# First layer's scales and shifts by packed matmuls with the weights moving, and the first value tiles projected beside the keys

## The chip, the core and the metric

The kernel runs on one core of a Trainium2 chip. The metric is the device time of one execution in microseconds; before the change it is 1470.97 us, the median of three runs (1470.38 to 1471.1).

## The reference, cut to what matters

Two layers over 1024 latent tokens and 256 context tokens of width 1024. Each layer scales and shifts its tokens by vectors made from a conditioning vector (`c` for the latents, `c_ctx` for the context), projects them, attends, gates, projects back and normalizes. The change concerns the first lines of the first layer:

```python
shift, scale, gate = jnp.split(silu_c @ w_ada[i] + b_ada[i], 3, axis=-1)
shift_c, scale_c, gate_c = jnp.split(silu_cc @ w_ada[i] + b_ada[i], 3, axis=-1)
u = h * (1.0 + scale[:, None, :]) + shift[:, None, :]
uc = hc * (1.0 + scale_c) + shift_c
...
q, k, v, g = _split_a(u @ w_in)
```

`w_ada[0]` is 1024 x 3072; shift and scale of the first layer are its first 2048 columns, 8.4 MB in f32, multiplied with only two vectors. Keys and values have 256 columns each.

## The kernel before

All is kept transposed: 1280 tokens in a row (three chunks of 512, 512 and 256, the last being the context), the 1024 features in 8 tiles (`KT`) of 128 partitions. A matmul with two f32 operands of full precision is made of three fp32r matmuls: both operands are split into a rounded high part and a rest (`uAh`, `uAl`; `wh`, `wl`; `wv` holds both for the values), and high x high, high x low and low x high are added up in PSUM.

The prologue is a loop over the 8 feature tiles. For each, `mod_mm` and `mod_end` make the tile's shift and scale for both vectors (`adc`), `u_make` scales and shifts the raw tokens (`hraw`) and splits them, and `k_mm` multiplies the tile into the keys' six accumulators: `kps` (four banks of PSUM) for the two halves of the keys and the first two chunks, `kc` for the context. Tile 0's shift and scale and the scales of tiles 2 and 4 to 7 come from matmuls with 128 x 128 pieces of the weights standing and the two vectors moving (8 for a column of 128 features, into `ada`). The rest are dot products: `scb` holds each vector spread over all partitions (by 16 transposes), and `dot` multiplies a 128 x 1024 tile of transposed weights with it, for one vector on DVE with its sum, for the other on POOL with the sum on ACT. `SDOTS` names the tiles whose scale is a dot product too.

Behind the loop the keys are evacuated (`rope_evac`: a shuffle, a product with `cos` on DVE, one with `sin` on POOL, an addition; then `k_store` splits them into a buffer `st` and stores that to `kdA` in DRAM). Beside it PE projects the values, 10 tiles of 128 tokens with 24 matmuls each; `v_evac` splits each pair of tiles into an `st` and stores it to `vdA`. There are two `st` buffers. Keys and values are read back (`kA`, `vA`) for the attention, whose first steps need the queries of the first pair of heads (`pj`, L207 to L209); scores are `S_A`, and DVE's L315 is the first step of the softmax. PSUM has four buffers of one bank (`psone`), which keys, value blocks and query chunks take in turn, and two of two banks (`psbig`).

Every engine works its own instructions in order. Their order is not the program's: a scheduler sets it when the kernel is built, within the dependencies. All DMAs are issued by one queue, SP. The weights pass through `Weights`: `load` issues the DMA, `split` makes the two parts on ACT (cast) and DVE or POOL (difference). Before the loop PE runs 12 matmuls of zeros (`warm`).

Of the kernel before, what the change touches and what calls it, by code (L numbers as in the profile page):

```python
# [37 lines left out]

SDOTS = (1, 3)
# [43 lines left out]
def build(tc, i, out):  # L83
# [23 lines left out]
    dma(ident, i["ident"])  # L107
    bad = cp.tile([P, 48], F32, name="bad")
    dma(bad, i["bada"])
    lnc = cp.tile([P, 2, KT], F32, name="lnc")  # L110
    dma(lnc, i["lnc"])
# [24 lines left out]
    class Weights:  # L136
# [8 lines left out]
        def load(self, upto):  # L145
            while self.nl < min(upto, self.cap):
                j = self.nl
                self.raw[j] = raw_tile(f"wr{j}")
                dma(self.raw[j], self.srcs[j])
                self.nl += 1  # L150

        def split(self, upto):
            while self.ns < min(upto, self.cap):
                j = self.ns
                self.load(j + 1)
                r = self.raw.pop(j)
                if 4 <= j < 8:
                    t = pp.tile([P, 2, 512], F32R, tag="wada", bufs=6, name=f"wv{j}")
# [4 lines left out]
                nc.scalar.copy(hi, r)  # L163
                e = nc.vector if j < 8 or j >= NA and j % 2 else nc.gpsimd
                e.tensor_tensor(lo, r, f32(hi), ALU.subtract)  # L165
                self.got[j] = (hi, lo)
                self.ns += 1
# [7 lines left out]
    add_w("Ak", [i["wAk"][nt, h] for h in range(2) for nt in range(2)])  # L175
    add_w("Av", [i["wAv"][q] for q in range(4)])
# [43 lines left out]
    def vproj_pieces(j0, u, evac):  # L220
# [4 lines left out]
        def piece(b, t, kq):  # L225
            def run():
                if b == 0 and t == 0 and kq == 0:
                    w.split(j0 + 4)
                    w.load(j0 + 6)
                if b == 4 and t == 1 and kq >= 2:  # L230
                    w.split(j0 + 4 + kq - 1)
                if t == 0 and kq == 0:
                    state["ps"] = psone(f"pv{j0}_{b}")
                pt = state["ps"][:, t * 256 : (t + 1) * 256]
                tok = slice((2 * b + t) * P, (2 * b + t + 1) * P)
                for kt in (2 * kq, 2 * kq + 1):
                    hi, lo = w.got[j0 + kt // 2]
# [3 lines left out]
                    mm(pt, lh, lo[:, sl], start=False, stop=False)  # L241
                    mm(pt, ll, hi[:, sl], start=False, stop=kt == KT - 1)  # L242
                if t == 1 and kq == 3:
                    evac(state["ps"], b)
# [3 lines left out]
        for b in range(5):  # L248
# [186 lines left out]
    dt, dt_st = pool("dots", "left")  # L435

    th0 = pp.tile([P, KT, 2], F32, name="th0")
    sil = pp.tile([P, KT, 2], F32, name="sil")
# [3 lines left out]
    wm = psone("warm")  # L442
    for _ in range(12):
        mm(wm, zero[:, 0:P], zero, start=True, stop=True)
    nc.scalar.activation(th0, cT, AF.Tanh, scale=0.5)
    nc.vector.scalar_tensor_tensor(sil, th0, 1.0, cT, ALU.add, ALU.mult)
    nc.vector.tensor_scalar(sil, sil, 0.5, None, ALU.mult)
# [33 lines left out]
    scb = [dt.tile([P, D], F32, name=f"scb{v}") for v in range(2)]  # L481

    def scb_make():
        for v in range(2):
            for hf in range(2):
                pb = psone(f"scb{v}_{hf}")
                for k in range(4):
                    c = sil[:, 4 * hf + k, v : v + 1].to_broadcast([P, P])
                    nc.tensor.transpose(pb[:, k * P : (k + 1) * P], c, ident)
                nc.scalar.copy(scb[v][:, HALVES[hf]], pb)  # L490

    def dot(t, v, acc, vec):
        if vec:
            o = dt.tile([P, D], BF16, tag="junk", bufs=1, name="junk")
            nc.vector.tensor_tensor_reduce(o, t, scb[v], 1.0, 0.0, ALU.mult, ALU.add, accum_out=acc)
        else:
            pr = dt.tile([P, D], F32, tag="prod", bufs=2, name="prod")
            nc.gpsimd.tensor_tensor(pr, t, scb[v], ALU.mult)
            nc.scalar.activation(pr, pr, AF.Copy, accum_out=acc)


    kps = {}
    kc = psbig("kc")
    raws, ada, wS = {}, {}, {}

    def mod_mm(kt):

        pa = ada[kt] = None if kt in SDOTS else psbig("ada")
        for x in (0, 1) if kt == 0 else () if kt in SDOTS else (1,):
            wt = pp.tile([P, KT, P], F32, tag="wada", bufs=6, name="wada")  # L510
            dma(wt, i["wadaC"][kt if x else KT])
            for kk in range(KT):
                mm(pa[:, 2 * x : 2 * x + 2], wt[:, kk, :], sil[:, kk, :], start=kk == 0, stop=kk == KT - 1)
        wS[kt] = []
        for x in () if kt == 0 else (0, 1) if kt in SDOTS else (0,):
            wS[kt].append(pp.tile([P, D], F32, tag="wada", bufs=6, name="wada"))
            dma(wS[kt][x], i["wadaS"][x, kt - 1])
        if kt == 0:
            scb_make()
            kps.update({(c, nt): psone(f"kp{c}_{nt}") for c in range(2) for nt in range(2)})  # L520
        raws[kt] = pp.tile([P, T], F32, tag="hraw", bufs=4, name="hraw")
        dma(raws[kt], i["hT"][:, kt, :])
        if kt in (0, 2):
            n = 2 if kt == 0 else 4
            w.load(n)
            w.split(n)

    def mod_end(kt):

        pa = ada.pop(kt)  # L530
        for x, t in enumerate(wS.pop(kt)):
            for v in (1, 0):
                dot(t, v, adc[:, kt, x, v : v + 1], v == 0)
        for x in range(2):
            src = adc[:, kt, x] if pa is None or kt and not x else pa[:, 2 * x : 2 * x + 2]
            nc.vector.tensor_scalar(adc[:, kt, x], src, bad[:, 8 * x + kt : 8 * x + kt + 1], None, ALU.add)
# [15 lines left out]
    def k_mm(kt):  # L552
        for c, (t0, n) in enumerate(CHUNKS):
            for nt in range(2):
                hi, lo = w.got[pos["Ak"] + 2 * (kt // 4) + nt]
                sl = slice((kt % 4) * P, (kt % 4 + 1) * P)
                rh, rl = uA.at(kt, slice(t0, t0 + n))
                pt = kps[c, nt] if c < 2 else kc[:, nt * 512 : nt * 512 + C]
                mm(pt, hi[:, sl], rh, start=kt == 0, stop=False)
                mm(pt, lo[:, sl], rh, start=False, stop=False)  # L560
                mm(pt, hi[:, sl], rl, start=False, stop=kt == KT - 1)
# [63 lines left out]
    for c, (t0, n) in enumerate(CHUNKS):  # L625
        for nt in range(2):
            pt = kps[c, nt] if c < 2 else kc[:, nt * 512 : nt * 512 + C]
# [3 lines left out]
    dt_st.close()  # L631
# [682 lines left out]
```

## Time and profile before

| | |
|---|---|
| median of three runs | 1470.97 us |
| profiled execution | 1475.79 us, span 1474.0 us |
| granted TensorE clock, mean | 0.983 |
| PE busy | 1403.7 us, 95% of the span |
| DVE, ACT, POOL busy | 1020.7, 744.0, 656.0 us |
| first key matmul | 17.07 us |
| first step of the keys' evacuation | 70.28 us |
| first query matmul | 101.19 us |
| first softmax step on DVE | 118.82 us |

The span runs from the first to the last instruction. In the timeline's rows the first number is the start in us, the second how long the instruction (or the merged group) lasted, and in brackets stands how long the engine was idle ahead and who ended that. [...] In a row of groups stand the count, the busy time, the mean in ns and the idle time ahead. In a row of waits stand the total, the count and the longest.

### The profile page before, as it was taken

The page shows a single profiled execution, that of the slowest core. Times are in us where ns is not written, and L with a number is a line of the kernel's source. Part 1 is how long each engine was busy: PE and PEld are TensorE (multiplying, and loading weights), DVE is VectorE, ACT ScalarE, POOL GpSimd, SP SyncE. Part 2 cuts the span into 40 slices and gives each one's busy share as a digit, 9 for nine tenths or more (in the row PEclk, how much of TensorE's full clock was granted, in tenths as well). Part 3 has the DMA queues.
Part 4 walks back from the last instruction along what each step waited for, and adds up shares of the span by engine and source line. Part 5 has one row for each costly group of instructions (what it writes and reads, how often), then busy time and mean ns, then how long its engine had stood idle before and what let it go on. Part 6 is the DMA issues. An engine that isn't in the chain of part 4 may idle for free.

```text
span 1474.0 us, 24907 instructions
## 1 busy us (share of the span) xinstructions
PE 1403.7 (95%) x8660; PEld 1231.2 (84%) x8660; DVE 1020.7 (69%) x2246; ACT 744.0 (50%) x1579; POOL 656.0 (45%) x787
## 2 busy tenths in 40 slices
PE   7898999999999999999999999999999999998995
PEld 5797888888888888788898889888998899877784
DVE  6957878788788788667532665655565555677788
ACT  4525676676767668533222444554454444466300
POOL 3434766566666657333211322332233323345564
PEclk7999999999999999999999999999999999999998
DMA  8455122222311213343268565555555465564443
GB/s 308 160 195 138 51 76 79 80 83 62 112 43 62 86 45 123 118 133 129 86 209 231 156 174 152 150 166 150 163 154 163 125 182 149 144 192 116 140 118 91
DMA packets 117229, 195.04 MB, mean 132 GB/s; under 512 B 9328, under 2 KB 57840, under 8 KB 117104
## 3 DMA queue, kind: packets, MB, share of 16 engines
q1 hardware_dynamic: 117104, 193.45, 43.9%
q8 instruction: 69, 1.13, 0.3%
q14 instruction: 56, 0.46, 0.1%
HBM read 141.51 MB, written 51.90 MB: 131 GB/s over the span
## 4 chain that ended last, share of the span: by engine, by line
PE 68%; DVE 14%; DMA 5%; ACT 5%; issue 5%; POOL 3%; SPq 0%; DVEq 0%; ACTq 0%; POOLq 0%
PE pj L208 8%; PE pj L207 8%; PE pj L209 8%; PE T_B L334 4%; PE T_A L334 4%; PE pvB L1054 3%; PE pvA L721 3%; PE pv L241 3%; PE pv L240 3%; PE pv L242 3%; PE S_A L692 3%; PE S_B L1023 2%; PE yA L419 2%; PE yA L418 2%; PE yA L417 2%
## 5 line engine op out<-in xcount | busy, mean ns | idle before, releaser
L327 POOL TENSOR_SCALAR s_B<-s_B,rs_B 128x640 f32<-128x640 f32 (+1 forms) x128 | 102.1, 798 | 308.1 <-DVE rs_B L326 270.1
L207 PE MATMUL pj<-uBh,wh 128*128 128x512 f32 (+1 forms) x448 | 177.1, 395 | 0.0
L208 PE MATMUL pj<-uBl,wh 128*128 128x512 f32 (+1 forms) x448 | 170.3, 380 | 0.0
L209 PE MATMUL pj<-uBh,wl 128*128 128x512 f32 (+1 forms) x448 | 169.8, 379 | 0.0
L322 ACT ACTIVATE s_A<-s_A,m_A 128x641 f32<-128x641 f32 (+2 forms) x160 | 119.5, 747 | 90.2 <-DVE m_A L315 74.3
L322 ACT ACTIVATE s_B<-s_B,m_B 128x640 f32<-128x640 f32 (+1 forms) x128 | 102.9, 804 | 121.4 <-DVE m_B L315 120.3
L340 DVE TENSOR_TENSOR pt_B<-T_B,pt_B 128x640 fp32r<-128x640 f32 (+1 forms) x128 | 100.9, 788 | 80.2 <-ACT pt_B L338 79.7
L327 POOL TENSOR_SCALAR s_A<-s_A,rs_A 128x640 f32<-128x640 f32 (+2 forms) x160 | 128.2, 801 | 57.4 <-DVE rs_A L326 54.9
L315 DVE CUSTOM_DVE_ANT_0 s_A<-S_A,msk,nsk 128x640 f32<-128x640 f32 (+2 forms) x160 | 123.7, 775 | 35.8 <-PE S_A L693 18.9
L207 PE MATMUL pj<-uAh,wh 128*128 128x512 f32 (+1 forms) x384 | 141.2, 368 | 0.0
L208 PE MATMUL pj<-uAl,wh 128*128 128x512 f32 (+1 forms) x384 | 138.4, 360 | 0.0
L209 PE MATMUL pj<-uAh,wl 128*128 128x512 f32 (+1 forms) x384 | 137.8, 359 | 0.0
L165 POOL TENSOR_TENSOR wl<-wr,wh 128x512 fp32r<-128x512 f32 x64 | 87.5, 1369 | 97.9 <-ACT wh L163 93.3
L340 DVE TENSOR_TENSOR ptl_A<-T_A,pth_A 128x640 fp32r<-128x640 f32 (+2 forms) x160 | 114.0, 712 | 13.5 <-PE pvA L721 7.0
L338 ACT CAST pt_B<-T_B 128x640 fp32r<-128x640 f32 (+1 forms) x128 | 84.4, 659 | 66.6 <-PE T_B L334 66.0
L334 PE MATMUL T_A<-ident,s_A 128*128 128x128 f32 x672 | 101.0, 275 | 11.0 <-DVE m_A L315 6.7
L334 PEld LDWEIGHTS T_A<-ident,s_A 128*128 128x128 f32 x672 | 77.5, 140 | 39.0 <-issue 16.3
L315 DVE CUSTOM_DVE_ANT_0 s_B<-S_B,bias 128x640 f32<-128x640 f32 (+1 forms) x128 | 100.4, 785 | 10.8 <-PE S_B L1024 9.4
L338 ACT CAST pth_A<-T_A 128x640 fp32r<-128x640 f32 (+2 forms) x160 | 96.4, 603 | 14.0 <-PE T_A L334 10.9
L334 PE MATMUL T_B<-ident,s_B 128*128 128x128 f32 x608 | 88.2, 274 | 13.7 <-DVE pt_B L340 9.5
L209 PEld LDWEIGHTS pj<-uBh,wl 128*128 128x128 f32 x448 | 84.4, 188 | 17.7
L334 PEld LDWEIGHTS T_B<-ident,s_B 128*128 128x128 f32 x608 | 70.0, 140 | 30.7 <-issue 13.5
(197 smaller groups left out, 3993.1 us busy)
## 6 DMA issues: line engine op xcount, KB each, us to landing
kB<-kdB SPq DMA_DIRECT2D x64, 320.0 KB, 5.3
gw<-in_wadaT SPq DMA_DIRECT2D x48, 256.0 KB, 2.8
vdB<-st SPq DMA_DIRECT2D x20, 512.0 KB, 3.1
vB<-vdB SPq DMA_DIRECT2D x16, 640.0 KB, 4.9
kdB<-st SPq DMA_DIRECT2D x16, 512.0 KB, 2.9
qdB<-st SPq DMA_DIRECT2D x16, 512.0 KB, 3.8
qB<-qdB SPq DMA_DIRECT2D x32, 256.0 KB, 4.6
ogr<-ogd SPq DMA_DIRECT2D x28, 256.0 KB, 3.0
```

The source lines that it names most:

```text
L165: e.tensor_tensor(lo, r, f32(hi), ALU.subtract)
L207: mm(pt[:, :n], hi[:, sl], rh, start=kt == 0, stop=False)
L208: mm(pt[:, :n], hi[:, sl], rl, start=False, stop=False)
L209: mm(pt[:, :n], lo[:, sl], rh, start=False, stop=kt == KT - 1)
L240: mm(pt, lh, hi[:, sl], start=kt == 0, stop=False)
L241: mm(pt, lh, lo[:, sl], start=False, stop=False)
L315: nc.vector.tensor_tensor_reduce(outp, sc, in1, scale, init if init is not None else 3e38, ALU.add, ALU.min, accum_out=s.m)
L322: nc.scalar.activation(s.t[:, :n], s.t[:, :n], AF.Exp, bias=s.m, scale=-1.0, accum_out=s.sum)
L327: nc.gpsimd.tensor_scalar(s.t[:, : s.w], s.t[:, : s.w], s.rs, 1.0, ALU.mult, ALU.mult)
L334: nc.tensor.transpose(tp[:, k * P : (k + 1) * P], s.t[:, src * P : (src + 1) * P], ident)
L338: nc.scalar.copy(pt.hi[:, :n, hl, :], tv)
L340: nc.vector.tensor_tensor(pt.lo[:, :n, hl, :], tv, f32(pt.hi[:, :n, hl, :]), ALU.subtract)
```

## The change

- All 16 columns of shift and scale come from matmuls with the weights moving. The two vectors stand as 32 columns (`sil`, two used, the rest zero); the weights (128 x 256: shift and scale of one feature tile) move. The eight parts of the sum over 1024 inputs are dealt to the four column groups of the array, two each (`tile_position`), so that group g's sum lands on partitions 32g to 32g+1 of `kc[:, 512:768]`. ACT copies these rows to SBUF (`rows`), and two small matmuls with the rows standing and a constant `sel` moving (ones on the partitions 32g and 32g+1) add the four groups and turn the result into columns. `sel` comes with the bias (`bada` has two columns more). One addition on DVE makes `adc`.
- The dot products, `scb`, their transposes and the pool `dots` are gone.
- The weights are loaded three tiles ahead (`mod_load`), ten buffers instead of six; key and value weights have four raw buffers of their own, and come in the order keys, values, keys, values.
- `v_mm` projects the first four token tiles of the values in the loop, one feature tile behind the keys, into a two-bank buffer `vps`; `vproj_pieces` starts at block 2.
- The four accumulators of the context keys move into one bank (`nt * C`), since the rows and sums take the other bank of `kc`.
- Eight more warming matmuls go into `vps` ahead of the first tile; the loads of `ident` and `lnc` move behind the loop.

```diff
+    def mod_load(kt):
+        wada[kt] = [pp.tile([P, 4, 2 * P], F32, tag="wada", bufs=10, name="wada") for _ in range(2)]
+        for hf in range(2):
+            dma(wada[kt][hf], i["wadaC"][kt, hf])
         raws[kt] = pp.tile([P, T], F32, tag="hraw", bufs=4, name="hraw")
         dma(raws[kt], i["hT"][:, kt, :])
...
+    def mod_rows(kt):
+
+        for hf, wt in enumerate(wada.pop(kt)):
+            for g in range(4):
+                gs = slice(32 * g, 32 * g + 32)
+                mm(kc[gs, 512:768], sil[:, 4 * hf + g, :], wt[:, g, :], start=hf == 0, stop=hf == 1, tile_position=(0, 32 * g))
+        rows[kt] = pp.tile([P, 2 * P], F32, tag="rows", bufs=2, name="rows")
+        nc.scalar.copy(rows[kt], kc[:, 512:768])
+
+    def mod(kt):
+
+        r = rows.pop(kt)
+        pa = kc[:, 768 + 4 * kt : 772 + 4 * kt]
         for x in range(2):
+            mm(pa[:, 2 * x : 2 * x + 2], r[:, x * P : (x + 1) * P], sel, start=True, stop=True)
+        nc.vector.tensor_tensor(
+            adc[:, kt],
+            pa.rearrange("p (x v) -> p x v", x=2),
+            bad[:, kt : kt + 9 : 8].unsqueeze(2).to_broadcast([P, 2, 2]),
+            ALU.add,
+        )
...
+    def v_mm(kt):
+        hi, lo = w.got[VALUES[kt // 2]]
+        sl = slice((kt % 2) * 256, (kt % 2 + 1) * 256)
+        for t in range(4):
+            lh, ll = uA.at(kt, slice(t * P, (t + 1) * P))
+            pt = vps[:, t * 256 : (t + 1) * 256]
+            mm(pt, lh, hi[:, sl], start=kt == 0 and t % 2 == 0, stop=False)
+            mm(pt, lh, lo[:, sl], start=False, stop=False)
+            mm(pt, ll, hi[:, sl], start=False, stop=kt == KT - 1 and t % 2 == 1)
+
+
+    upto = (3, 4, 6, 7, 8)
     for kt in range(-1, KT + 1):
         if kt + 1 < KT:
-            mod_mm(kt + 1)
-        if 0 <= kt < KT:
-            u_make(kt)
-        if kt + 1 < KT:
-            mod_end(kt + 1)
+            for n in range(3) if kt < 0 else (kt + 3,) if kt + 3 < KT else ():
+                mod_load(n)
+                w.load(upto[min(n, 4)])
+            mod_rows(kt + 1)
         if kt > 0:
             k_mm(kt - 1)
-        if kt == KT - 2:
-            w.split(8)
+        if kt + 1 < KT:
+            mod(kt + 1)
+        if kt < 0:
+
+            warm(vps[:, 0:512], 8)
+        if kt > 0:
+            v_mm(kt - 1)
+        if kt < KT and kt >= 0:
+            u_make(kt)
+            w.split(upto[min(kt, 4)])
+    dma(ident, i["ident"])
+    dma(lnc, i["lnc"])
     dma(cos, i["cos"])
     dma(sin, i["sin"])
...
+    for b in range(2):
+        v_evac(pp, vdA)(vps[:, b * 512 : (b + 1) * 512], b)
+    merge([], vproj_pieces(-1, uA, v_evac(pp, vdA), 2))
-    merge([], vproj_pieces(pos["Av"], uA, v_evac(pp, vdA)))
```

How the built order of instructions changes, in three places. On PE, the second and third tile's work before: `ada` is the pair of vectors, `kp` and `kc` are the keys' accumulators.

```order
L559 MATMUL kp_1_199<-uAh_108,wh_210 128x512
L560 MATMUL kp_1_199<-uAh_108,wl_211 128x512
L561 MATMUL kp_1_199<-uAl_111,wh_210 128x512
L513 MATMUL ada<-sil,wada 128x2 x8
L559 MATMUL kc<-uAh_109,wh_206 128x256
L560 MATMUL kc<-uAh_109,wl_207 128x256
```

On PE from the first tile's last key matmuls on, now: L503 are the packed matmuls, L512 the two small ones, L541 to L543 the keys.

```order
L503 MATMUL kc<-wada,sil 32x256 x4
L542 MATMUL kp_1_147<-uAh_106,wl_236 128x512
L543 MATMUL kp_1_147<-uAl_109,wh_235 128x512
L512 MATMUL kc<-bad,rows 128x2 x2
L541 MATMUL kp_0_146<-uAh_106,wh_231 128x512
L542 MATMUL kp_0_146<-uAh_106,wl_232 128x512
L541 MATMUL kp_1_147<-uAh_106,wh_235 128x512
L541 MATMUL kp_0_144<-uAh_105,wh_231 128x512
L542 MATMUL kp_0_144<-uAh_105,wl_232 128x512
L503 MATMUL kc<-wada,sil 32x256 x4
```

The packed matmuls of a tile stand in two groups of four among key matmuls, and right behind the two small matmuls of the second tile stands the first key matmul on that tile's tokens (`uAh_106`).

On DVE behind the last tile, before: `uAl` is the last part of the tokens, `wv` a split of value weights, L463 to L466 and L475 the keys' evacuation.

```order
L550 TENSOR_TENSOR uAl_112<-hraw,uAh_109 128x256
L463 STREAM_SHUFFLE rb<-kp_0_196 128x512
L464 TENSOR_TENSOR ra<-kp_0_196,cos 128x512
L463 STREAM_SHUFFLE rb<-kp_1_197 128x512
L165 TENSOR_TENSOR wv_557<-wr_555,wv_557 128x512
L165 TENSOR_TENSOR wv_562<-wr_560,wv_562 128x512
L577 TENSOR_SCALAR nsk<-nsk 128x16
L466 TENSOR_TENSOR ra<-ra,rb 128x512
```

And now, with L467 to L470 and L479 in their place:

```order
L532 TENSOR_TENSOR uAl_110<-hraw,uAh_107 128x256
L580 TENSOR_SCALAR nsk<-nsk 128x16
L467 STREAM_SHUFFLE rb<-kp_0_144 128x512
L468 TENSOR_TENSOR ra<-kp_0_144,cos 128x512
L467 STREAM_SHUFFLE rb<-kp_1_145 128x512
L470 TENSOR_TENSOR ra<-ra,rb 128x512
L468 TENSOR_TENSOR ra<-kp_1_145,cos 128x512
```

The two splits of value weights no longer stand between the first two key results.

On SP around the first stores of keys, before (`wr` are raw weights of queries and gates):

```order
L149 DMA wr_666<-in_wAq 128x512
L476 DMA kdA<-st 128x2x512
L149 DMA wr_964<-in_wAg 128x512
L149 DMA wr_970<-in_wAg 128x512
L476 DMA kdA<-st 128x2x512 x2
L149 DMA wr_976<-in_wAq 128x512
L149 DMA wr_978<-in_wAq 128x512
L476 DMA kdA<-st 128x2x512
```

And now:

```order
L146 DMA wr_929<-in_wAg 128x512
L480 DMA kdA<-st 128x2x512
L146 DMA wr_935<-in_wAq 128x512
L146 DMA wr_937<-in_wAq 128x512
L480 DMA kdA<-st 128x2x512 x3
L480 DMA kdA<-st 128x2x256 x2
L266 DMA vdA<-st 128x2x512 x5
```

One pair of loads stands behind the first store instead of a pair behind the first and another behind the third; the eleven stores themselves and their order stay.

More of the change, by code (lines that the diff above doesn't have):

```diff
@@ L106, in build @@
     dma(cT, i["cT"])
-    dma(ident, i["ident"])
-    bad = cp.tile([P, 48], F32, name="bad")
+    bad = cp.tile([P, 50], F32, name="bad")
     dma(bad, i["bada"])
+    sel = bad[:, 48:50]
     lnc = cp.tile([P, 2, KT], F32, name="lnc")
-    dma(lnc, i["lnc"])
     half = cp.tile([P, 1], F32, name="half")
@@ L246, in piece @@
             return (6 * 109, run)
[L248 removed]
+        for b in range(b0, 5):
             for t in range(2):
@@ L478, in k_store @@
         return store
[L481 to L499, printed above, removed]
@@ L502, in build @@
-    kps = {}
-    kc = psbig("kc")
[L504 to L520, printed above, removed]
+    kps = {(c, nt): psone(f"kp{c}_{nt}") for c in range(2) for nt in range(2)}
```

70 lines of the change are left out of this document (31 added, 39 removed).

## The prediction

> **What bounds the kernel now.** The sums below are made in the profiled execution (1475.79 us, of which 1474.0 are the span), which is 4.8 us longer than the median of the runs, 1470.97; I carry the difference that I find over to the median. A change of 0.2%, 2.9 us, is about what a measurement of this kernel can tell from none.
>
> I read the page's first part first, then the table of stretches over the first 130 us, since the change touches nothing later.
>
> ```profile
> PE 1403.7 (95%) x8660; PEld 1231.2 (84%) x8660; DVE 1020.7 (69%) x2246; ACT 744.0 (50%) x1579; POOL 656.0 (45%) x787
> ...
> 0.00:14.00 14.00, 10.83 (x60) 7.52 (x60) 2.66 (x8) 4.46 (x7) 2.01 (x5) 1.00 0.79 290
> 14.00:22.00 8.00, 1.81 (x3) 0.80 (x4) 8.00 (x8) 4.67 (x9) 5.45 (x3) 0.50 0.83 300
> 22.00:34.00 12.00, 12.00 (x40) 10.36 (x41) 11.53 (x18) 4.03 (x8) 5.45 (x2) 0.50 0.94 336
> ...
> 46.00:52.00 6.00, 6.00 (x20) 4.84 (x19) 5.55 (x9) 2.79 (x7) 3.08 (x1) 0.54 0.63 228
> ```
>
> PE sets the kernel's time everywhere but here. In these rows (busy time of PE, PEld, DVE, ACT, POOL, then clock, DMA share, GB/s) PE idles 6 of 8 us, and its clock is 0.50 for 20 us and 0.54 for another 6, while DVE is nearly full. The groups and waits of the first 70 us say what DVE does:
>
> ```profile
> L495 DVE CUSTOM_DVE_ANT_0 junk<-wada,scb 128x1024 bf16<-128x1024 f32 x9 | 13.0, 1446 | 0.1
> L536 DVE TENSOR_SCALAR adc<-adc,bad 128x2 f32<-128x2 f32 x9 | 9.8, 1098 | 0.0
> ...
> ACT hraw L545 <- DVE adc L536: 24.5, 8, 5.7
> ```
>
> The dot products hold DVE 13.0 us, the two-element additions behind them 9.8, and ACT waits 24.5 us for the sums before it can build the next tokens. All these go.
>
> Behind the prologue the chain runs over small steps, so I read the timeline of DVE, SP and PE there.
>
> ```profile
> 70.28 0.74 DVE L463 STREAM_SHUFFLE rb<-kp 128x512 f32<-128x512 f32 x1
> ...
> 73.26 1.37 DVE L165 TENSOR_TENSOR wv<-wr,wv 128x512 fp32r<-128x512 f32 x1 [0.32 <-ACT wv L163]
> ...
> 74.63 0.68 DVE L466 TENSOR_TENSOR ra<-ra,rb 128x512 f32<-128x512 f32 x1
> ...
> 80.02 1.57 SPq L149 DMA_DIRECT2D wr<-in_wAg  x2
> 81.82 4.07 SPq L476 DMA_DIRECT2D kdA<-st  x2
> ...
> 101.19 0.39 PE L207 MATMUL pj<-uAh,wh 128*128 128x512 f32 x1
> ...
> 106.61 0.42 DVE L264 SCALAR_TENSOR_TENSOR st<-pv,st 128x256 fp32r<-128x256 f32 x1 [0.45 <-ACT st L263]
> ...
> 107.52 2.59 SPq L666 DMA_DIRECT2D kA<-kdA  x4
> ...
> 112.27 0.74 DVE L463 STREAM_SHUFFLE rb<-pj 128x512 f32<-128x512 f32 x1
> ...
> 115.64 0.28 PE L692 MATMUL S_A<-kA,qA 128*128 128x256 f32 x1
> ...
> 118.38 0.42 DVE L648 TENSOR_TENSOR qA<-pj,qA 64x256 fp32r<-64x256 f32 x1
> 118.82 0.75 DVE L315 CUSTOM_DVE_ANT_0 s_A<-S_A,msk,nsk 128x512 f32<-128x512 f32 x1
> ...
> ACT st L474 <- DMA kdA<-st: 6.6, 3, 4.1
> ...
> ACT st L263 <- DMA vdA<-st: 5.7, 2, 3.4
> ```
>
> Eleven results (six of keys, five of values) leave through two buffers `st`, each held until its store to DRAM has landed. This chain begins with the first key result at 70.28 and ends at 107.03 (106.61 + 0.42); only then are the keys read back, and DVE reaches the first softmax at 118.82, 48.5 us after the chain's start. It runs beside PE's values, and it is what the prologue's end hands its time to.
>
> **The change part by part.** *Removed:* all dots on POOL, DVE and ACT, and their additions; the 7 tiles that PE multiplied with weights standing; 16 transposes. *The new prologue* is limited, I think, by PE, which works its rows in order. Prices of its matmuls:
>
> ```profile
> 56.02 0.39 PE L560 MATMUL kp<-uAh,wl 128*128 128x512 f32 x1
> 56.24 0.39 PE L561 MATMUL kp<-uAl,wh 128*128 128x512 f32 x1
> 56.47 0.28 PE L559 MATMUL kc<-uAh,wh 128*128 128x256 f32 x1
> 56.59 0.28 PE L560 MATMUL kc<-uAh,wl 128*128 128x256 f32 x1
> ...
> 57.19 1.84 PE L513 MATMUL ada<-sil,wada 128*128 128x2 f32 x16
> ...
> 98.10 0.28 PE L241 MATMUL pv<-wv,uAh 128*128 128x256 f32 x1
> 98.22 0.28 PE L242 MATMUL pv<-wv,uAl 128*128 128x256 f32 x1
> ```
>
> Start to start: 0.227 us with 512 columns, 0.117 with 256, 0.118 for values. The `ada` row counts 16 where the program has 8: a plain f32 matmul runs as two, 0.115 us each with only two columns.
>
> Start: the first weights were used at 7.25 and then the second tile; two small loads no longer stand ahead of them (0.48 us each by the rows below), so I put both tiles at 7.6, the new matmuls, the copy, the small pair and the addition at 10, and 4 us for tokens and the key weights' cast. Before, it was 12.07 (first addition) to 17.07, 5 us. The first key matmul thus starts at 14 instead of 17.07.
>
> ```profile
> 2.12 0.43 SPq L111 DMA_DIRECT2D lnc<-in_lnc  x1
> 2.59 0.91 SPq L511 DMA_DIRECT2D wada<-in_wadaC  x2
> ...
> 7.25 1.85 PE L513 MATMUL ada<-sil,wada 128*128 128x2 f32 x16
> ...
> 12.07 0.35 DVE L536 TENSOR_SCALAR adc<-ada,bad 128x2 f32<-128x2 f32 x2 [8.06 <-PE ada L513]
> ...
> 17.07 0.80 PE L559 MATMUL kp<-uAh,wh 128*128 128x512 f32 x1 [5.03 <-ACT uAh L549]
> ```
>
> From there to the first finished key result:
> - keys: 8 tiles of 12 long and 6 short matmuls, less the 15 that follow that result: 87 x 0.227 + 42 x 0.117 = 24.6 us.
> - values beside them: 7 tiles x 12 x 0.118 = 9.9 us.
> - packed scales: 8 matmuls a tile, 7 tiles, a price that no row shows. Cheap end: each of the 16 halves streams 256 columns once (0.117) and four groups share that time, 0.47 us a tile. Dear end: every half streams them twice (0.227) and nothing overlaps, 3.6. I take 16 x 0.117 = 1.87, which is also what two streams at half overlap give, because the two halves of one group follow each other and only neighbouring groups can overlap: 13.1 us, about what the 1.84 of the removed row costs.
> - small pairs: 7 x 4 x 0.115 = 3.2 us.
> - waits: in the first two tiles the order puts a matmul on fresh tokens right behind the small pair, which costs the addition, the scaling and a cast, about 1.8 us (by the rows below 61.20 to 62.38 for addition and scaling, and the first cast of three in 1.43): 3.6 us.
> - clock: PE may idle some 2.4 us ahead of the first key matmul, and the rows of 14 to 34 and 46 to 52 us show what idling does: 6 us at 0.54 lose 2.8. I put in 1.7, as the new idle is half as long as the 5.03 before.
>
> ```profile
> 61.20 0.22 DVE L536 TENSOR_SCALAR adc<-ada,bad 128x2 f32<-128x2 f32 x1
> ...
> 61.66 0.87 DVE L547 TENSOR_SCALAR hraw<-hraw,adc 128x512 f32<-128x512 f32 x2
> ...
> 62.38 1.43 ACT L549 CAST uAh<-hraw 128x512 fp32r<-128x512 f32 x3
> 63.02 1.63 DVE L550 TENSOR_TENSOR uAl<-hraw,uAh 128x512 fp32r<-128x512 f32 x3 [0.48 <-ACT uAh L549]
> ...
> DMA packets 5261, 16.56 MB, mean 237 GB/s; under 512 B 960, under 2 KB 1088, under 8 KB 5257
> ```
>
> Sum: 14 + 24.6 + 9.9 + 13.1 + 3.2 + 3.6 + 1.7 = 70.1, against 70.28: a gain of 0.2, with 60 and 82 at the ends of the packed price. Loads don't set this: even the 16.56 MB that all of the first 70 us moved are 49 us at the 336 GB/s of 22 to 34 us, and the last tile's weights are wanted after 55. DVE needs 0.22 + 0.87 + 1.63 = 2.7 us a tile of the 7 that PE takes, ACT 2.2 (from 61.66 to the last cast's end) and the new copy of 256 columns out of PSUM, so both hide; if PE got much faster, the loads would be late next. SP now waits twice for a split value weight ahead of later tiles' loads; three tiles of lead cover it. The loads of `ident` and `lnc` go behind the last tile's, and `ident` is first used by the transposes behind 118.82.
>
> *Behind it:* four of ten value tiles are done, so PE has 6 x 24 x 0.118 = 17.0 us to the queries instead of 28.3 (11.3 less). But their results still pass the two buffers behind the keys: eleven stores, no fewer. The chain loses the value-weight splits in DVE's queue between key results (some 2.4 us up to 74.63) and the loads at 80.02 on SP ahead of the second store (others take their place behind the first store); I put it at 35 us instead of 36.75. PE reaches the second query chunk 26 us after the first key result and waits to about 30 for a PSUM bank that value block 2 holds; then 5.4 us of matmuls (24 x 0.227), 6.1 of evacuation (112.27 to 118.38). Reading the keys back takes 8.1 (107.52 to 115.64). The first softmax comes at 44.5 to 47 after the chain's start; I take 45.8, a gain of 2.7. The new stall is 4 us of PE between queries; what PE saved there is spent waiting.
>
> Total 0.2 + 2.7, or 3: 1471 - 3 = 1468 us.
>
> [...]
>
> **The rivals.** *Full packing:* the four groups run side by side even though each has two halves, two rounds of two halves that stream twice, 8 x 0.117 = 0.94 us a tile. That saves 6.5 us: 1461.5. For: the groups write different quarters; against: matmuls start in order. [...]
> *No packing (slower):* the groups run one behind the other with two passes, 3.6 us a tile: 12.1 us more, 1480. It decides from 2.3 us a tile, where the 3 us are used up. For: nothing in the trace shows an overlap of two matmuls' columns.
> *Cold clock:* the idle stretch before the first key matmul drops the clock to 0.50 and, as from 22 to 34, the packed matmuls with few columns don't raise it: 6 us instead of 1.7, 1472.3. Against: twenty warming matmuls and a wait half as long as the 5.03 of before.
> *The chain isn't the bound:* if the two buffers turn over faster, PE's 11.3 us come through: the queries would start at 70.1 + 4.1 + 17.0 = 91.2 instead of 101.19, 1461. Against: the waits for `kdA` and `vdA` stores.
>
> **How the numbers follow.** Forecast 0.37 (its own range 1463 to 1474: faster 0.20, same 0.11, slower 0.06); full packing 0.20; free chain 0.06; no packing 0.22; cold clock 0.15 (same 0.03, slower 0.12). Faster 0.46, same 0.14, slower 0.40. The range must reach both full and no packing, since each has a fifth, and 2 us on either side for the chain's uncertain 44.5 to 47 and the cheap end: 1458 to 1482.
>
> **What would show it.** Right: the packed matmuls of a tile take about 1.9 us, the first key shuffle lies near 70, PE's clock stays at 1.00 from 14 on, a stall of some 4 us between query chunks with DVE's value evacuations late, and the first softmax 46 us after the first key shuffle. Wrong: the first shuffle before 65 or after 75; PE waiting for loads in the prologue; queries without a stall.

## The result and the profile after

The changed kernel takes 1466.19 us (median of 12 runs, 1460.94 to 1468.33), the kernel before, run beside it, 1472.25 us (12 runs). The ratio is 0.9952, with an interval of 0.994 to 0.9964: 0.5%, or 6.1 us, faster. The forecast was 1468, in a range of 1458 to 1482. The profiled execution of the changed kernel took 1466.38 us, at its median; that of before took 1475.79, 3.5 us above its own. So of the 9.4 us between the two spans about 3.5 are the execution's, not the kernel's.

The first part of the page, and the table of stretches over the prologue, in the same columns as before (PE, PEld, DVE, ACT, POOL, clock, DMA share, GB/s):

```profile
PE 1399.2 (96%) x8700; PEld 1216.0 (83%) x8700; DVE 989.2 (68%) x2220; ACT 734.7 (50%) x1565; POOL 631.1 (43%) x779
```

PE is busy for 4.5 us less than before, the other three engines for 9 to 32 us less; a matmul at half clock counts with all the time that it takes. Then the stretches:

```profile
14.00:22.00 8.00, 6.32 (x42) 3.06 (x40) 2.66 (x6) 2.52 (x5) 0.00 (x0) 0.91 1.03 407
22.00:34.00 12.00, 10.32 (x65) 6.62 (x60) 4.46 (x9) 4.08 (x8) 0.00 (x0) 0.86 0.45 169
```

From 14 to 22 us PE is now busy for 6.32 us instead of 1.81 and the clock is 0.91 instead of 0.50; DVE, which was full there, works 2.66. From 34 us on PE is full at full clock (12.00 of the 12 us from 34 to 46, clock 1.00). PE sets the prologue's pace, as forecast.

The timeline of PE, DVE and SP, with the places of which the prediction spoke:

```profile
11.91 1.74 PE L541 MATMUL kp<-uAh,wh 128*128 128x512 f32 x3 [2.57 <-ACT wh L160]
...
68.94 0.73 DVE L467 STREAM_SHUFFLE rb<-kp 128x512 f32<-128x512 f32 x1
...
90.20 0.39 PE L206 MATMUL pj<-uAh,wh 128*128 128x512 f32 x1
94.88 0.42 DVE L264 SCALAR_TENSOR_TENSOR st<-pv-1_2_738,st 128x256 fp32r<-128x256 f32 x1 [0.45 <-ACT st L263]
95.65 0.39 PE L206 MATMUL pj<-uAh,wh 128*128 128x512 f32 x1
...
99.89 0.41 DVE L264 SCALAR_TENSOR_TENSOR st<-pv-1_4_848,st 128x256 fp32r<-128x256 f32 x1
...
111.52 0.75 DVE L315 CUSTOM_DVE_ANT_0 s_A<-S_A,msk,nsk 128x512 f32<-128x512 f32 x1 [2.47 <-PE S_A L697]
```

The first key result comes at 68.94 instead of 70.28 (1.3 earlier), the queries at 90.20 instead of 101.19, the chain through the two buffers ends at 100.30 instead of 107.03, and the first softmax step comes at 111.52 instead of 118.82: 7.3 us earlier. The second query chunk starts at 95.65 with no idle time ahead, where the prediction had a stall of 4 us: value block 2 had left its bank at 95.30. SP stood for 13.9 us (15.62 to 29.54) ahead of a load of value weights, whose raw buffer wasn't free, and the lead of three tiles covered it: up to 70 us no wait of PE was for a load.

The time gained grows behind that point. The store of the first head pair's output, in the timeline of SP, before and then after:

```profile
201.41 0.33 SPq L738 DMA_DIRECT2D ogd<-gA  x1
```

```profile
187.70 0.33 SPq L742 DMA_DIRECT2D ogd<-gA  x1
```

That is 13.7 us earlier, almost twice the softmax's 7.3. What the time up to there consists of, before and then after, in the columns of the stretches (PE's busy time is the first number behind the length, the clock the third from the end):

```profile
0.00:201.41 201.41, 180.54 (x1085) 156.88 (x1086) 149.42 (x289) 102.83 (x215) 95.12 (x100) 0.92 0.49 161
```

```profile
0.00:187.70 187.70, 174.97 (x1125) 141.77 (x1126) 119.39 (x263) 93.23 (x201) 70.67 (x92) 0.98 0.50 173
```

PE idles 12.7 us instead of 20.9. (The rows of PE overlap: a long matmul's lasts 0.39 us, and the next starts 0.227 later; prices of matmuls are from start to start.) And of its busy time 23.4 us ran at half clock before (within 13.9 to 34.4, 44.7 to 51.5 and 130.0 to 133.4) and 6.8 now (12.0 to 15.4 and 29.0 to 32.4); as a long matmul then takes 0.43 us from start to start instead of 0.227, that is 8.3 us of delay less. Together that is 16.5 us; the work that PE does up to there grew by 2.8. So the gain is idle time and half clock, not less work for PE.

Why it isn't over at the softmax, the groups of PE's long `pj` matmuls between the queries' start and the end of the first softmax step show. First before (101 to 119.6 us), then after (90 to 112); each row has a count, the busy time and the mean in ns:

```profile
L207 PE MATMUL pj<-uAh,wh 128*128 128x512 f32 x19 | 7.4, 390 | 0.0
```

```profile
L206 PE MATMUL pj<-uAh,wh 128*128 128x512 f32 x27 | 10.5, 390 | 0.0
```

With the two rows that belong to each (18 and 18 before, 26 and 26 after), 55 long matmuls had started by the end of that step before and 79 now; 48 of them are queries. The 24 more are gate projections that PE works while it waits for the keys to come back. They are needed in any case, so 24 x 0.227 = 5.4 us of work leave the time behind the softmax.

### The profile page after: what moved, and what is told of

Same layout as the page of the kernel before. It is cut to its first block, busy times and chain, and to the rows that moved or that the text cites. A ratio compares the mean times of both kernels' runs of the same rounds, so it can differ in the third digit from the quotient of the medians.

```text
span 1464.6 us, 24919 instructions
## 1 busy us (share of the span) xinstructions
PE 1399.2 (96%) x8700; PEld 1216.0 (83%) x8700; DVE 989.2 (68%) x2220; ACT 734.7 (50%) x1565; POOL 631.1 (43%) x779
## 4 chain that ended last, share of the span: by engine, by line
PE 70%; DVE 11%; DMA 5%; issue 5%; ACT 4%; POOL 3%; SPq 0%; DVEq 0%; ACTq 0%; POOLq 0%
PE pj L207 9%; PE pj L208 8%; PE pj L206 8%; PE T_B L334 4%; PE T_A L334 4%; PE pvB L1058 3%; PE pvA L725 3%; PE S_A L696 2%; PE pv L240 2%; PE pv L242 2%; PE pv L241 2%; PE S_B L1027 2%; DMA gwB<-in_wadaT 2%; PE yA L419 2%; PE yA L418 2%
## 5 line engine op out<-in xcount | busy, mean ns | idle before, releaser
L315 DVE CUSTOM_DVE_ANT_0 s_B<-S_B,bias 128x640 f32<-128x640 f32 (+1 forms) x128 | 100.3, 784 | 10.8 <-PE S_B L1028 9.9
```

Of the source, the lines that this page charges most:

```text
L315: nc.vector.tensor_tensor_reduce(outp, sc, in1, scale, init if init is not None else 3e38, ALU.add, ALU.min, accum_out=s.m)
```

## The experiments

All ratios are to the kernel before, run beside each; its medians there were 1472.06 (the first four kernels), 1473.39 and 1471.66 us. "The changed kernel" is the one of the result.

**One column group.** The eight packed matmuls of a tile all go to column group 0, in a single sum; everything else stays.

```diff
+    mm(kc[:, 512:768], zero[:, 0:P], zero[:, 0:256], start=True, stop=True)
...
-                gs = slice(32 * g, 32 * g + 32)
-                mm(kc[gs, 512:768], sil[:, 4 * hf + g, :], wt[:, g, :], start=hf == 0, stop=hf == 1, tile_position=(0, 32 * g))
+                kk = 4 * hf + g
+                mm(kc[0:32, 512:768], sil[:, kk, :], wt[:, g, :], start=kk == 0, stop=kk == 7, tile_position=(0, 0))
```

> The eight packed matmuls of a tile all go to column group 0, one behind the other, with all else as in the changed kernel. Theory A (the groups really run side by side, and PE's work in the prologue is on the path): a half takes 0.107 us or more instead of 0.071, a tile 0.6 us more if each half streams its 256 columns once, 2.3 us more if twice; seven tiles make the kernel 4 or 16 us longer, 1470 or 1482. Theory B (no overlap is at work, a half simply costs 0.07): unchanged, 1466. Theory C (overlap, but the chain of two store buffers or the loads set the end): the rows get longer and the time stays within 1 us of 1466.

It takes 1474.27 us, ratio 1.0017 (1.0007 to 1.0027): the whole gain is gone. (Its profiled execution took 1478.12 us, 3.9 above that median.) In the timeline of PE of the changed kernel a packed group (eight halves, two in each column group) stands like this among key matmuls:

```profile
57.53 0.39 PE L541 MATMUL kp<-uAh,wh 128*128 128x512 f32 x1
57.85 0.64 PE L503 MATMUL kc<-wada,sil 128*32 128x256 f32 x8
58.42 0.50 PE L542 MATMUL kp<-uAh,wl 128*128 128x512 f32 x1
58.76 0.39 PE L543 MATMUL kp<-uAl,wh 128*128 128x512 f32 x1
```

and all sixteen halves of a tile, one behind the other, in the same view of this kernel:

```profile
53.86 3.64 PE L504 MATMUL kc<-wada,sil 128*32 128x256 f32 x16
57.43 0.50 PE L542 MATMUL kp<-uAh,wh 128*128 128x512 f32 x1
...
77.82 0.73 DVE L467 STREAM_SHUFFLE rb<-kp 128x512 f32<-128x512 f32 x1
```

Alone, a half costs 3.57 / 16 = 0.223 us, the 0.227 of the prediction's dear end, about twice the 0.117 of an ordinary matmul with 256 columns. Packed, eight halves cost 58.42 - 57.85 = 0.57 us, 0.071 each, so the four groups overlap 3.1 times. That is 2.4 us a tile; seven tiles would be 17 us, and the first key result comes 8.9 us later. The other 8 are covered: between 8 and 70 us PE idles 1.1 us instead of 5.9, and the clock was 1.00 in all that time, where the changed kernel loses 3.4 us to half speed.

**Values behind the loop.** In the program the four value tiles stand behind the keys' loop.

```diff
-        if kt > 0:
-            v_mm(kt - 1)
...
+    for kt in range(KT):
+        v_mm(kt)
```

> The values' first four token tiles are projected behind the loop instead of beside the keys (same matmuls, same PSUM); the scales stay packed. Theory A (PE's total work up to the attention decides; it is full from 34 to 117 us in the changed kernel): the first key shuffle comes some 6 to 9 us earlier (60 to 63 instead of 68.9), but PE now idles in the prologue on fresh tokens and loads, so the whole gets longer by that idle time, 0 to 5 us: 1466 to 1471. Theory B (the prediction's: the chain through two store buffers, begun by the first key result, decides): the first softmax comes 6 to 8 us earlier than 111.5 and the kernel is faster, 1459 to 1461.

1470.31 us, 0.9983 (0.9967 to 0.9999), some 4 us slower than the changed kernel. The built order follows the edit only in part: the scheduler pulls values back among the keys, from 35.14 us on instead of 28.90, and of the 84 value matmuls that the changed kernel works ahead of the first key result 52 are still ahead of it. So this run tells what later values cost, not what the loop takes without them. The stretch from 22 to 34 us:

```profile
22.00:34.00 12.00, 10.32 (x54) 5.65 (x54) 5.16 (x11) 4.09 (x8) 0.00 (x0) 0.78 0.26 95
```

And the timeline of PE and DVE:

```profile
35.14 0.28 PE L551 MATMUL vps<-wv,uAh 128*128 128x256 f32 x1
...
68.38 0.73 DVE L467 STREAM_SHUFFLE rb<-kp 128x512 f32<-128x512 f32 x1
...
114.83 0.75 DVE L315 CUSTOM_DVE_ANT_0 s_A<-S_A,msk,nsk 128x512 f32<-128x512 f32 x1
```

The 32 matmuls that moved are 32 x 0.118 = 3.8 us, yet the first key result comes only 0.6 us earlier: the clock from 22 to 34 us is 0.78 where it was 0.86, and up to there 13.7 us run at half clock instead of 6.8, and what is left out is paid again behind the loop. The first softmax is 3.3 us later. The values early beside the keys are worth their place as work that keeps PE going.

**Standing weights.** All tiles' scales and shifts by the old form: 128 x 128 pieces of weights standing, two vectors moving; no packing, no rows, no small pair.

```diff
+        for x in range(2):
+            for kk in range(KT):
+                wt = rows[kt, kk // 4]
+                mm(pa[:, 2 * x : 2 * x + 2], wt[:, kk % 4, x * P : (x + 1) * P], sil[:, kk, 0:2], start=kk == 0, stop=kk == 7)
```

> The scales and shifts come from plain matmuls with the weights standing and the two vectors moving (16 a tile, 32 halves at 0.115 us by the row of before), without packing, copy of rows and small pairs; the values stay beside the keys. Theory A (PE's work decides): 3.7 us a tile instead of 1.1 + 0.4 + changes of mode, some 2 us more for seven tiles and 1 at the start, 1480. Theory C (the chain or the loads decide): less than 5 us more, below 1471.

1488.63 us, 1.0112 (1.0097 to 1.0127): 22 us over the changed kernel, 9 more than expected. (What the expectation calls changes of mode are the steps around a packed group, 0.32 us going in and 0.34 coming out in the changed kernel's timeline above, where ordinary long matmuls start 0.227 apart.) The timeline of PE, and then the stretches, the first of them up to the first key result at 93.10:

```profile
54.68 2.73 PE L506 MATMUL kc<-sil,wada 128*128 128x2 f32 x24
57.27 0.37 PE L539 MATMUL kc<-uAh,wh 128*128 128x256 f32 x1
```

```profile
8.00:93.10 85.10, 81.60 (x467) 74.30 (x467) 25.91 (x56) 21.90 (x41) 0.00 (x0) 0.76 0.48 186
54.50:57.90 3.40, 3.40 (x31) 3.35 (x30) 0.00 (x0) 0.00 (x0) 0.00 (x0) 1.00 0.15 50
57.90:61.40 3.50, 3.50 (x11) 2.83 (x11) 2.48 (x6) 2.67 (x5) 0.00 (x0) 0.51 1.01 360
```

The matmuls themselves cost (57.27 - 54.68) / 24 = 0.108 us a half, near the 0.106 of before from start to start; the clock is what was missed. From 8 us to that result its mean is 0.76 (0.94 in the changed kernel), though PE idles only 3.5 us of it: from 54.50 to 57.90 PE is busy throughout, 2.6 us of it with two-column matmuls, and the next 3.4 us run at half clock.

**Filled idle time.** 22, 12 and 12 matmuls on zeros (256 bf16 columns of `rows` moving, result unused) in the three stretches where PE waits for the key weight's cast and twice for fresh tokens.

```diff
+            if kt < 0:
+                warm(vps[:, 0:512], 8)
+            r = rows[kt + 1].bitcast(BF16)[:, 1::2]
             mod(kt + 1)
-        if kt < 0:
-
-            warm(vps[:, 0:512], 8)
+            for _ in range({-1: 22, 0: 12, 1: 12}.get(kt, 0)):
+                mm(vps[:, 0:256], zero[:, 0:P], r, start=True, stop=True)
```

> Matmuls of the new rows with zeros fill three of PE's idle stretches (2.57, 1.68 and 1.68 us ahead of fresh tokens in the first three tiles); the order of all else stays. Theory A (PE's work decides and the two half-speed stretches of 3.4 us each at 12 and 29 us cost 3.4 us of it): the clock stays at 1.00 from 6 us on, first key shuffle 65.5 instead of 68.9, kernel 2 to 4 us faster, 1462 to 1464. Theory C (loads or the chain decide): the clock stays up and the time stays within 1 us.

1459.15 us, 0.9909 (0.9895 to 0.9924); once more, beside the two-filling kernel below, 1459.16 us, 0.991 (0.9894 to 0.9927). It beats the kernel before by 13 us and the changed kernel by 6 to 7 (by 5 to 6 against the changed kernel's second series below). The stretch from 14 to 22 us, and the timeline of DVE and SP:

```profile
14.00:22.00 8.00, 7.70 (x56) 4.47 (x55) 3.32 (x8) 2.52 (x5) 0.00 (x0) 1.00 1.03 407
```

```profile
67.36 0.73 DVE L467 STREAM_SHUFFLE rb<-kp 128x512 f32<-128x512 f32 x1
...
99.40 0.41 DVE L264 SCALAR_TENSOR_TENSOR st<-pv-1_4_894,st 128x256 fp32r<-128x256 f32 x1
110.97 0.75 DVE L315 CUSTOM_DVE_ANT_0 s_A<-S_A,msk,nsk 128x512 f32<-128x512 f32 x1 [2.47 <-PE S_A L699]
...
187.13 0.33 SPq L744 DMA_DIRECT2D ogd<-gA  x1
```

The clock is 1.00 throughout and the first key result 1.6 us earlier. But the first output store is only 0.6 us ahead of the changed kernel's 187.70. The spans of the two profiles differ by 5.1 us (1459.5 and 1464.6), so 4.5 of the gain lie later, where behind the prologue the order of the instructions is the same on every engine.

> The filled kernel once more, unaltered, to stand beside the run with two fillings on the same chip and to give a second profile. Expected: 1458 to 1461, no half-speed stretch in the prologue; whether there is one in the second layer (the changed kernel had one in each of its two profiles, at different places, the filled one none) tells whether the filling spares it or the one profile was lucky.

The second profile of the filled kernel had the prologue at full clock again. It had one stretch at half clock near 611 us (0.60 from 610 to 614), so the first profile's having none was partly luck.

**The changed kernel again.**

> The changed kernel once more, unaltered, for a second profile. In its first profile it was 13.8 us ahead of the kernel before at 160 us and only 9.6 at the end; the code of the second layer is the same in both. Theory A: the part given back between 790 and 960 us is chance of that execution (half-speed stretches of TensorE fall differently each time); a second profile gives it back at other places or by another amount, differing by 2 us or more at the end. Theory B: it belongs to the changed kernel's timing (loads or buffers met later); then the same 4 us go in the same place again. Time 1464 to 1468 either way.

1464.9 us, 0.9946 (0.9925 to 0.9966), span 1462.7. A stretch of the second layer in the changed kernel's first profile, then one in this profile, both of the same code in the same order:

```profile
855.00:862.00 7.00, 4.79 (x18) 3.84 (x18) 5.62 (x13) 2.40 (x5) 1.96 (x2) 0.76 0.60 201
```

```profile
736.00:744.00 8.00, 6.13 (x37) 6.06 (x38) 2.22 (x9) 0.75 (x2) 0.00 (x0) 0.79 0.89 259
```

In the first profile the half clock falls behind a wait at 855 (the clock from 736 to 744 is 1.00 there), in the second behind one at 736 (1.00 from 855 to 862). So which of these waits costs the clock changes from one execution to the next. That there is a loss in this part of the second layer doesn't change: both profiles have it, as is shown further down.

**Three store buffers** in the filled kernel; the room comes from a narrower table of zeros.

```diff
-        return pl.tile([P, 2, 512], F32R, tag="st", bufs=2, name="st")
+        return pl.tile([P, 2, 512], F32R, tag="st", bufs=3 if pl is pp else 2, name="st")
```

> The filled kernel with three store buffers instead of two for the keys' and values' way out (room for it comes from a table of zeros cut from 512 to 448 columns, so the warming matmuls have 448). Theory A (the prediction's: eleven stores through two buffers set when the keys can be read back): the chain from the first key shuffle to its last evacuation falls from 31 us to 27 or less, the first softmax comes 3 to 5 us sooner, and the time falls by 3 to 5, to 1455. Theory B (the first softmax no longer decides, since PE pulls gate matmuls ahead while it waits): the softmax comes sooner but PE has as much work left, and the time stays within 1 us of the filled kernel's 1459.

1460.63 us, 0.9921 (0.9906 to 0.9936): not faster than with two. The timeline of DVE and SP:

```profile
94.36 0.43 DVE L264 SCALAR_TENSOR_TENSOR st<-pv-1_4_894,st 128x256 fp32r<-128x256 f32 x1 [0.45 <-ACT st L263]
106.10 0.75 DVE L315 CUSTOM_DVE_ANT_0 s_A<-S_A,msk,nsk 128x512 f32<-128x512 f32 x1
187.47 0.33 SPq L744 DMA_DIRECT2D ogd<-gA  x1
```

The chain ends 5.0 us sooner (94.79, 99.81 with two buffers), the softmax starts 4.9 us sooner, and the first output store comes at 187.47, where the filled kernel with two buffers had 187.13. The softmax's start isn't what the time hangs on. What PE doesn't do ahead of the softmax it does behind it: 55 long `pj` matmuls start ahead of the softmax here and 77 with two buffers, 22 x 0.227 = 5.0 us of work, which is what the softmax gained.

**Without the additional warming matmuls** (the eight ahead of the first tile, of the changed kernel).

```diff
-            warm(vps[:, 0:512], 8)
+            pass
```

> The changed kernel without its eight additional warming matmuls ahead of the first feature tile. Theory A (the rival of the cold clock: activity ahead of the first key matmul decides whether the prologue starts at full speed): one or two more half-speed stretches of 3.4 us each, of which each loses about 1.7 us, ahead of 30 us; first key shuffle at 70 to 72 instead of 68.9, time 2 to 4 us above the changed kernel's. Theory B: the two idle stretches behind them halve the clock anyway; the first key shuffle stays within 0.5 us and the time within 1 us.

1462.64 us, 0.9934 (0.9917 to 0.9952): no slower than the changed kernel in the same series (1464.9). The half clock covers 9.3 to 16.1 us instead of 12.0 to 15.4, most of the additional time while PE waits for the key weight's cast, and the first key result comes at 67.83. The eight matmuls buy nothing.

**Two fillings.** The filled kernel without the eight warming and the 22 filling matmuls ahead of the first key matmul.

```diff
-                warm(vps[:, 0:512], 8)
+                pass
...
-            for _ in range({-1: 22, 0: 12, 1: 12}.get(kt, 0)):
+            for _ in range({0: 12, 1: 12}.get(kt, 0)):
```

> The filled kernel without anything between the first tile's small pair and the first key matmul: the eight additional warming matmuls and the 22 filling ones there are left out, the 12 and 12 in the two later idle stretches stay. The wait ahead of the first key matmul (2.6 us for the key weight's cast) is open again. Theory A (only the later idle matters, since the first key matmul waits for the cast in any case and came 1.3 us later behind the filling): first key matmul at 11.7 to 11.9, one half-speed stretch ahead of 16 us and none behind it, first key shuffle at 66 to 67.4, time within 1 us of the filled kernel's 1459. Theory B (the first idle stretch leaves the clock low and the loss returns): half-speed stretches also behind 16 us, first key shuffle at 68 or later, time 2 to 4 us above the filled kernel's.

1460.37 us, 0.9922 (0.9907 to 0.9937), within 1.2 us of the filled kernel beside it, with the earliest key result and store of all these kernels. The timeline of DVE and SP:

```profile
66.72 0.73 DVE L467 STREAM_SHUFFLE rb<-kp 128x512 f32<-128x512 f32 x1
...
185.49 0.33 SPq L744 DMA_DIRECT2D ogd<-gA  x1
```

The half clock lasts from 11.2 to 18.0 us (the clock from 14 to 22 us is 0.75), over the first tile's work, and costs nothing that shows; behind it there is none in the prologue. The 24 matmuls in the two later waits do the work of all 46.

## Why the prediction was right, step by step

**Direction and size.** Right: 1468 forecast, 1466.19 measured, with the largest chance on faster (0.46, and 0.40 on slower). That the two lie 1.8 us apart is in part luck. Several terms were mis-sized, in both directions, and nearly cancel; the step that carries the gain on behind the prologue failed; and of the 13.7 us that the kernel had gained at its first output store a part is given back in the second layer, of which the prediction says nothing.

**The start.** Forecast 14, measured 11.91. The addition was done at 9.16 instead of 10 (9.00 and 0.16 long on DVE), and the tokens and the key weight's cast took 2.75 us instead of the 4 put in; the cast came last.

**Packed scales.** Forecast 1.87 us a tile. A group costs 0.57 and the ordinary matmuls on either side start 0.32 (57.53 to 57.85) and 0.34 (58.42 to 58.76) apart instead of 0.227, so 0.57 + 0.09 + 0.11 = 0.77 a group and 1.54 a tile, 10.8 us for seven instead of 13.1. The rival of full packing came nearest for the matmuls themselves: 1.14 a tile measured, 0.94 by the rival, and a half by itself does take as long as two streams of 256 columns, 0.223 us with one column group against 2 x 0.117. The half overlap behind the 1.87, by which only neighbouring groups can overlap, was the author's estimate; no run shows it: it makes 8 x 0.117 = 0.94 us for the eight halves of a group, and they took 0.57. The rival of no packing is the kernel with one column group, and it did come out slower than before, by 2 us instead of the rival's 9, since idle time and clock absorbed part.

**The steps around a packed group.** The prediction's sum has no term for them. They are 0.09 us longer going in and 0.11 coming out, 4 x 7 x 0.10 = 2.8 us in all. Not all of that belongs to packing: behind the plain f32 matmuls of the kernel before, which aren't packed, the step behind the first ordinary matmul is longer too, as PE's timeline before shows:

```profile
57.19 1.84 PE L513 MATMUL ada<-sil,wada 128*128 128x2 f32 x16
58.89 0.48 PE L559 MATMUL kp<-uAh,wh 128*128 128x512 f32 x1
59.20 0.39 PE L560 MATMUL kp<-uAh,wl 128*128 128x512 f32 x1
```

From 58.89 to 59.20 are 0.31 instead of 0.227, 0.08 more; going in no step is longer (57.06 to 57.19). So only the 0.09 going in, and 0.02 or 0.03 coming out, belong to the packed groups alone. What causes these longer steps no run shows.

**Small pairs and waits.** The two waits on fresh tokens were 1.68 us each (forecast 1.8), the small pairs 0.36 each (61.72 to 62.08; forecast 0.46 a tile). The prediction's 0.115 a half is the length of a row divided by its 16; from start to start it is 1.70 / 16 = 0.106 (57.19 to 58.89 above). But the step behind a small pair is longer, 0.20 instead of 0.118. The timeline of PE:

```profile
61.72 0.50 PE L512 MATMUL kc<-bad,rows 128*128 128x2 f32 x4
62.08 0.36 PE L552 MATMUL vps<-wv,uAh 128*128 128x256 f32 x1
62.28 0.28 PE L553 MATMUL vps<-wv,uAl 128*128 128x256 f32 x1
```

**Clock.** Forecast 1.7 us lost, measured 3.4: two stretches of 3.4 us at half speed, one behind the first wait and one behind the third. "PE's clock stays at 1.00 from 14 on" was wrong.

With the measured terms the sum is 11.9 + 24.6 + 9.9 + 10.8 + 2.5 + 3.4 + 3.4 = 66.5, against 68.94 for the first shuffle. Of the 2.4 left over 0.6 are the longer steps behind the seven small pairs; the rest isn't assigned.

**Behind the prologue.** The chain took 31.4 us, not 35, and the first softmax came 42.6 us after its start, not 45.8. The step that failed is the last sentence of that part, "what PE saved there is spent waiting". There was no stall between query chunks, which the prediction had named as a sign of being wrong, and where PE did have to wait for the chain, the built order put gate projections there. The kernel with three store buffers shows, for the filled kernel, that the chain didn't set the time: 4.9 us off the softmax's start, none off the time. So the rival in which the chain isn't the bound, given a chance of 0.06, is the better description: the first store of output came 13.7 us earlier.

**Where the rest went.** The changed kernel leads by 13.7 us at 188 us, by 14.6 at the second layer's first store of keys (728.73 before), by 11.6 at that layer's first output store (905.00 before) and by 9.4 at the end of the spans; the medians differ by 6.1. Of the 9.4, 3.5 are the profiled execution of before, which stands that much above its median. What is given back falls in the second layer. SP's timeline there, of the changed kernel and then of the filled one:

```profile
714.12 5.90 SPq L917 DMA_DIRECT2D kdB<-st  x2
...
893.40 0.33 SPq L1073 DMA_DIRECT2D ogd<-gB  x1
```

```profile
713.06 5.90 SPq L919 DMA_DIRECT2D kdB<-st  x2
...
888.41 0.33 SPq L1075 DMA_DIRECT2D ogd<-gB  x1
```

Between the two stores lie 179.3 us in the changed kernel, 178.1 in its second profile and 179.9 without the additional warming, but 175.4, 174.2, 174.6 and 175.2 in the four profiles with filled waits (176.3 before). The first three have one or two steps at half clock in this stretch and 5.4 to 6.2 us of idle PE, the filled ones none and 3.2 to 4.2. But for the three-buffer kernel (174.6) the order of the instructions behind the prologue is the same in all of these seven. So this isn't the chance of one execution: without filling some 3 to 6 us more go there each time, 3.9 of the 5.1 us between the first profiles of the changed and the filled kernel. (With one column group, values behind and standing weights, each in an order of its own, the stretch took 179.7, 177.3 and 176.9 us.) Why stays open. One of the waits is PE's at 736 us for the cast of a weight, 1.2, 2.3 and 2.7 us without filling and 0.5, 0.4 and 1.3 with two buffers and filling, and no run tells why.

## What to carry to other kernels

Price a prologue by the engine that works its rows in order: its work, its waits, and what the waits cost in clock. Here two of the three (2.57, 1.68 and 1.68 us) were followed by 3.4 us at half clock, 1.7 us lost each. Work that is needed later anyway, such as a projection of the next stage, helped to keep the engine going (6.8 us at half clock up to the first key result, 13.7 where part of the values moved behind the loop); matmuls on zeros did it too (clock 1.00 from 14 to 22 us instead of 0.91). Look in the built order whether the scheduler put that work where the program has it. Before a chain behind a stage is called the bound, ask what the engine beside it can pull forward while the chain runs: a milestone that comes earlier, such as the first softmax, is a gain only if less work is left behind it.

## What the hardware showed beyond the expected

**Half clock in steps of 3.4 us.** In these profiles the clock changes on a grid of 3.4 us: before, half clock lasts from 13.9 to 34.4, from 44.7 to 51.5 and from 130.0 to 133.4, six, two and one times 3.41; after, from 12.0 to 15.4 and from 29.0 to 32.4, and the two begin five times 3.41 apart. Behind most steps in which PE was idle for more than about half the time the clock stood at 0.50. The stretches of the changed kernel, cut on that grid:

```profile
8.60:12.00 3.40, 0.83 (x6) 0.33 (x5) 2.48 (x6) 2.81 (x6) 0.00 (x0) 1.00 1.05 421
12.00:15.40 3.40, 3.40 (x13) 1.54 (x13) 1.38 (x3) 0.38 (x1) 0.00 (x0) 0.50 1.02 408
...
18.80:22.20 3.40, 1.97 (x14) 1.07 (x14) 2.51 (x6) 2.15 (x4) 0.00 (x0) 1.00 1.04 404
22.20:25.60 3.40, 3.40 (x27) 2.22 (x24) 0.00 (x0) 0.37 (x1) 0.00 (x0) 1.00 0.52 208
25.60:29.00 3.40, 1.72 (x11) 1.42 (x10) 2.41 (x6) 2.73 (x6) 0.00 (x0) 1.00 0.00 0
29.00:32.40 3.40, 3.40 (x12) 1.94 (x11) 2.05 (x4) 0.97 (x2) 0.00 (x0) 0.51 0.52 182
```

Busy for 0.83 or 1.72 of 3.4 us: the next step is at half speed. Busy for 1.97: it isn't, although the wait inside was the same 1.68 us long, cut differently by the grid. In the second profile a step busy for 1.53 us (736.0 to 739.4) was followed by one at 0.50 and one busy for 2.05 (855.1 to 858.5) by one at 1.00. In the whole profiles of before and of the changed kernel, the first 4 and the last 20 us left out, every step at full clock busy for 1.50 us or less was followed by one at 0.50, and none busy for more than 1.8 was. Between 1.5 and 2 us both occur: with the values behind a step busy for 1.52 (106.2 to 109.6) was followed by one at 0.51 and without the additional warming one busy for 1.90 (23.0 to 26.4) by one at 0.50, while in the changed kernel one busy for 1.68 (1302.2 to 1305.6) was followed by one at 1.00. Of the way back two steps tell: with two fillings a step at half speed that was busy for 2.50 us (11.2 to 14.6) was followed by another at 0.50, without the additional warming one that was busy for 3.22 (26.4 to 29.8) by one at 1.00.

**Half clock behind two-column matmuls.** In the kernel with standing weights a step in which PE was busy throughout, 2.6 us of it with matmuls of two columns (54.50 to 57.90, shown there), was followed by one at half clock (0.51 from 57.90 to 61.40). Matmuls with 256 columns moving and 32 standing did keep the clock up: with one column group, where they run for 3.6 us in a row, it was 1.00 from 8 to 70 us.

**Overlap of column groups.** Four groups of plain f32 matmuls, two halves each, ran 3.1 times as fast as in one group (0.071 against 0.223 us a half), though in the built order each group's two halves follow each other.
